# One 512-column product for both token parts in the mixers, gates and branches of a two-block layer

## The chip, the cores and the metric

The kernel runs on one core of a Trainium2 chip. The metric is the device time of one execution in microseconds; less is better. The engines are named as in the profile: PE is TensorE (its weight loads are listed as PEld), DVE is VectorE, ACT is ScalarE, POOL is GpSimd, SP issues most of the DMAs.

## The reference

256 tokens of width 2048 pass through two blocks in float32.

```python
def first_block(x, ...):
    proj = rms_norm(x, g_mix) @ w_in
    y_dsa  = dsa_mixer(q, k, v, q_idx, k_idx, w_idx)      # 8 heads, keys picked by an indexer
    y_rwkv = rwkv7_mixer(r, d_w, k, v, d_a, d_g)          # 16 heads, recurrence over the tokens
    x = x + concat([y_dsa, y_rwkv]) @ w_out
    return x + hier_moe(rms_norm(x, g_ffn), ...)          # 16 experts, group routing

def second_block(x, ...):
    proj = rmsnorm(x, norm1_g) @ w_in                     # columns: u, v | s5 | q, k, v | 3 x 2048 gates
    gates = sigmoid(proj[..., o_c:] + b_gate)
    y_a = gmlp_mixer(uv); y_b = s5_mixer(s5_in); y_c = stick_breaking_attention(q, k, v)
    br = einsum('blnw,nwd->blnd', stack([y_a, y_b, y_c]), w_branch)
    x = x + sum(gates * br) @ w_out
    x = x + square(relu(rmsnorm(x, norm2_g) @ w_mlp_in)) @ w_mlp_out
    return rmsnorm(x, final_g)
```

`s5_mixer` ends with `g * sigmoid(g @ w_glu + b_glu)`. Inside `rwkv7_mixer` the columns r, k and v are first mixed with those of the token before.

## The kernel before, in words

**Products in two parts.** Each float32 operand of a large product is split into a high part, rounded for the fast matmul, and a low part, the rest. `load_split` loads a chunk of weights (`raw`, 4 x 128 rows by 256 columns), ACT copies it into the high part (`wh`, L211) and DVE subtracts for the low part (`wl`, L212). `wh` and `wl` have three buffers each. A chunk is called a split below. The tokens are split once per block into `hx`, where for each of 16 row tiles the high 256 columns and the low 256 columns lie side by side.

**`ws_steps`** computes 256 output columns for the 256 tokens. For each row tile `k` and each of two pieces of 128 output columns it makes three products of 256 columns: `wh` with the high tokens, `wh` with the low tokens, `wl` with the high tokens. Both pieces lie in the halves of one PSUM bank (`acc`, four banks). A caller reads that bank with one DVE instruction.

**`wide_group`**, used in the MLP alone before, gives each piece a bank of its own. `wh` goes with high and low tokens side by side in one product of 512 columns, and `wl` with the high tokens in one of 256, which is added to the bank's first half. The bank's second half is then copied by ACT (`lo`, L2122) and added to the first by DVE (`r`, L2123).

**The order.** The code runs as generators: a stream of dense groups (`rkv`, `scores`, `attend` and, in block 2, `U`, `C`, `Q`, `gate`) yields after each row tile, and side chains (the rwkv chunks, attention heads, the s5 states) are advanced between the yields. A scheduler then lays all instructions out for each engine, and every engine works through its own list in order.

**Places that the prediction speaks of.** At the end of block 1 the last rwkv pair, the last attention heads and the output product (`acc<-wh,yx`) meet; then the router turns 16 tiles of the residual (`mx<-cst_cg,xr`, L1202), copies each with ACT or DVE (`hT`) and multiplies it by the router's weights (`mx<-wr,hT`). In block 2, `s5` first computes its tables on DVE (from `xm` to `ek` and `bb`), then its pool "s5" is opened with a load of `cc` on POOL's queue, and 32 states follow, each with products on PE, a scan on DVE and multiplications on POOL (`b`, `z`, `tab`, `sl`). The last product of a state is `mx<-sl,Ch`.

Of the kernel before, what the change touches and what calls it, by code (L numbers as in the profile page):

```python
# [18 lines left out]
T = 256  # L19
# [94 lines left out]
class Ker:  # L114
# [152 lines left out]
    def wide_group(self, ap, xx):  # L267
# [11 lines left out]
        return banks  # L279

# [181 lines left out]
    def mixers1(self, y, st):  # L462
# [46 lines left out]
        self.hhl = (hh, hl)  # L509

# [22 lines left out]
        def rkv(n, off, j):  # L533
            v, b = yield from self.ws_steps([(w_in[:, R0 + off + 256 * j:R0 + off + 256 * (j + 1)], 0)], 256,
                                            hh, hl, [(0, 128), (128, 128)])
            ready[n, j] = self.shift(wp, v, [mu("mu_" + n, 2 * j + i) for i in range(2)],
                                     128, bank=b[0], name=n)
# [110 lines left out]
    def shift(self, pool, views, mus, m, bank=None, name="lo"):  # L648
# [4 lines left out]
        p = bank.rearrange("p (a t) -> p a t", a=2) if n == 2 else views[0][:, None, :]  # L653
        pn = pool.tile([128, 2, T], F32, name="shn")
        nc.vector.tensor_mul(pn[:m, :n], p[:m], self.row[:m, :n])
# [284 lines left out]
    def dsa(self, y, st, chains):  # L940
        nc, A, c, par = self.nc, self.A, self.c, self.par
        hh, hl = self.hhl
        w_in = A["w_in"][0]
# [12 lines left out]
        def turned(bank, n, h, scale=1.0, src=None):  # L956
# [5 lines left out]
            for a in range(0, 128, h):  # L962
                b = a ^ h
                o, f = slice(a, a + h), slice(b, b + h)
                nc.scalar.activation(sw[o, :n * T], bank[f], AF.Copy, scale=scale if scale == 1.0 else scale[f])
            if src is bank:
                nc.scalar.activation(src, src, AF.Copy, scale=scale)
# [18 lines left out]
        two = [(0, 128), (128, 128)]  # L986
# [32 lines left out]
        def scores(j):  # L1019
            v, bk = yield from self.ws_steps([(w_in[:, 3072 + 256 * j:3328 + 256 * j], 0)], 256, hh, hl, two)  # L1020
            chains.append(scores_chain(j, bk))

        def scores_chain(j, bk):
            src, sw = turned(bk[0], 2, 32)
# [38 lines left out]
        def attend(j):  # L1063
            qk = []
            for base, gain, nm in ((0, "q_gain", "qr"), (1024, "k_gain", "kr")):
                v, bk = yield from self.ws_steps([(w_in[:, base + 256 * j:base + 256 * (j + 1)], 0)], 256, hh, hl, two)
                chains.append(qk_chain(bk, gain, nm, qk))
            chains.append(heads_chain(j, qk))

        def qk_chain(bk, gain, nm, qk):  # L1070
            src = d2.tile([128, 2 * T], F32, name="rsrc")
            nc.vector.tensor_mul(src.rearrange("p (a t) -> p a t", a=2), bk[0].rearrange("p (a t) -> p a t", a=2), self.row)
# [429 lines left out]
    def block2(self):  # L1502
        nc, A, tc = self.nc, self.A, self.tc
        w_in = A["w_in_2"][0]
        two = [(0, 128), (128, 128)]
        with ExitStack() as st:
# [5 lines left out]
            hh, hl = self.hhl  # L1512
# [6 lines left out]
            def gate(d, pool, n, ci):  # L1519
# [3 lines left out]
                v, bk = yield from self.ws_steps([(w_in[:, c0:c0 + 256], 0)], 256, hh, hl, two)  # L1523
                nc.vector.tensor_mul(*(t.rearrange("p (a t) -> p a t", a=2) for t in (g, bk[0])), row)
# [62 lines left out]
            yh = q.tile([128, 24, T], F32R, name="y2h")  # L1587
            yl = q.tile([128, 24, T], F32R, name="y2l")
# [7 lines left out]
            def glu():  # L1596
                g = q.tile([128, KD, T], F32R, name="gs", tag="ml")
                gh, gl = g[:, 0:8], g[:, 8:16]
# [3 lines left out]
                for j in range(4):  # L1602
                    v, bk = self.ws_group([(A["s5_w_glu_2"][0, :, ts(j, 256)], 0)], 256,
                                          [gh[:, k] for k in range(8)], [gl[:, k] for k in range(8)], two)
# [4 lines left out]
                    sg = q.tile([128, 2, T], F32, name="sgl", tag="m", bufs=2)  # L1609
                    for i in range(2):  # L1610
                        ct = 2 * j + i
                        nc.scalar.activation(sg[:, i], v[i], AF.Sigmoid, bias=par["b_glu"][:, ct:ct + 1])
# [598 lines left out]
```

## Time and profile before

| what | value |
|---|---|
| median of 3 runs | 2908.3 us (2908.26 to 2910.01) |
| the profiled execution's own time | 2907.5 us |
| its span | 2905.7 us |
| PE busy | 2837.3 us, 98% |
| DVE, ACT, POOL busy | 69%, 56%, 13% |

The time is 1.8 us more than the span, which runs from the first instruction to the end of the last. Busy shares are means over stages with different limits, so a stage is read from its own stretch.

### The profile page before, as it was taken

The numbers are of one execution on the slowest core, as the hardware profiler recorded it, in microseconds if no ns is written. First come the engines' busy times: TensorE is split into PE (matmuls) and PEld (weight loads), VectorE is DVE, ScalarE is ACT, GpSimd is POOL, SyncE is SP. The second block draws the span as 40 slices with busy tenths as digits, with TensorE's granted clock in tenths as the row PEclk, the third lists the DMA queues.
The fourth block names the chain that finished last, engine by engine and source line by source line (L and its number), as shares of the span: only waits on it lengthen the run. The fifth ranks groups of instructions, "written<-read, shape, count | busy, mean of one in ns | idle before, by whom it ended". The sixth has DMA issues, their size and how long they took to land.

```text
span 2905.7 us, 45911 instructions
## 1 busy us (share of the span) xinstructions
PE 2837.3 (98%) x17602; PEld 2511.7 (86%) x17602; DVE 2009.7 (69%) x2807; ACT 1628.0 (56%) x2225; POOL 371.6 (13%) x645
## 2 busy tenths in 40 slices
PE   8999999997999999999999999999999999999998
PEld 8998989876888788888878999999988888888887
DVE  7685876656898899987787866555555654456554
ACT  6455466546777777766555464444445543355443
POOL 2111111011000000015998400000000000000000
PEclk9999999998999999999999999999999999999999
DMA  7444443483989999945334456666656666666665
GB/s 204 130 117 120 118 119 100 134 278 128 372 297 338 378 382 359 381 141 165 117 105 131 140 172 186 186 189 184 187 184 199 189 189 195 192 187 187 191 193 172
DMA packets 400515, 576.68 MB, mean 198 GB/s; under 512 B 25064, under 2 KB 252656, under 8 KB 400160
## 3 DMA queue, kind: packets, MB, share of 16 engines
q1 hardware_dynamic: 397632, 567.74, 60.5%
q0 software_dynamic: 2624, 5.93, 0.7%
q8 instruction: 139, 2.28, 0.3%
q14 instruction: 88, 0.72, 0.1%
q10 hardware_dynamic: 32, 0.01, 0.0%
HBM read 571.51 MB, written 2.10 MB: 197 GB/s over the span
## 4 chain that ended last, share of the span: by engine, by line
PE 48%; POOL 6%; DVE 1%; DMA 1%; issue 0%; ACT 0%; ACTq 0%; POOLq 0%
PE acc L221 46%; PE mx L221 1%; POOL ttmp L1998 1%; POOL ttmp L2001 1%; POOL tab L1999 1%; POOL tab L2002 1%; POOL tab L2000 1%; POOL b L2037 1%; POOL z L2038 0%; POOL tab L1997 0%; POOL sl L2050 0%; DVE wl L212 0%; DMA raw<-in_w_in_dram 0%; DMA cc<-in_s_c_im_dram 0%; POOL cf L1981 0%
## 5 line engine op out<-in xcount | busy, mean ns | idle before, releaser
L212 DVE TENSOR_TENSOR wl<-raw,wh 128x1024 fp32r<-128x1024 f32 (+1 forms) x917 | 1123.6, 1229 | 651.7 <-ACT wh L211 630.2
L211 ACT ACTIVATE wh<-raw 128x1024 fp32r<-128x1024 f32 (+1 forms) x917 | 965.4, 1055 | 900.8 <-PE acc L221 718.8
L221 PE MATMUL acc<-hx,wh 128*128 128x256 f32 (+3 forms) x5280 | 1144.3, 306 | 1.7 <-ACT wh L211 1.1
L221 PEld LDWEIGHTS acc<-hx,wh 128*128 128x128 f32 (+2 forms) x5280 | 844.9, 188 | 55.2 <-issue 8.0
L221 PE MATMUL acc<-hx,wl 128*128 128x256 f32 x3152 | 886.8, 283 | 1.1 <-DVE wl L212 1.1
L221 PEld LDWEIGHTS acc<-hx,wl 128*128 128x128 f32 x3152 | 591.2, 188 | 9.9 <-issue 4.3
L212 DVE TENSOR_TENSOR wl<-rx,wh 128x1024 fp32r<-128x1024 f32 x159 | 191.4, 1223 | 26.8 <-ACT wh L211 18.5
L221 PE MATMUL acc<-wl,xgh 128*128 128x512 f32 x512 | 203.0, 398 | 1.7 <-DVE wl L212 1.4
L221 PE MATMUL acc<-wh,xgh 128*128 128x512 f32 x512 | 201.4, 394 | 2.2 <-ACT wh L211 2.1
L221 PE MATMUL acc<-wh,xgl 128*128 128x512 f32 x512 | 201.5, 394 | 0.0
L221 PE MATMUL acc<-wh,al 128*128 128x512 f32 x512 | 199.2, 389 | 0.0
L221 PE MATMUL acc<-wh,ah 128*128 128x512 f32 x512 | 199.2, 389 | 0.0
L211 ACT ACTIVATE wh<-rx 128x1024 fp32r<-128x1024 f32 x159 | 167.5, 1060 | 56.4 <-PE acc L221 38.4
L221 PE MATMUL acc<-wl,ah 128*128 128x512 f32 x512 | 179.2, 389 | 0.0
L221 PE MATMUL mx<-wh,act 128*128 128x512 f32 x512 | 138.1, 390 | 1.5 <-DVE act L218 0.8
L221 PE MATMUL acc<-wh,hx 128*128 128x512 f32 x384 | 128.7, 416 | 0.8 <-ACT wh L211 0.8
L221 PEld LDWEIGHTS acc<-wl,xgh 128*128 128x128 f32 x512 | 96.3, 188 | 26.0 <-DVE wl L212 5.5
L221 PEld LDWEIGHTS acc<-wh,xgh 128*128 128x128 f32 x512 | 96.3, 188 | 23.9 <-ACT wh L211 4.1
L221 PEld LDWEIGHTS mx<-wh,act 128*128 128x128 f32 x512 | 95.8, 188 | 22.2 <-DVE act L218 1.2
L221 PEld LDWEIGHTS acc<-wh,xgl 128*128 128x128 f32 x512 | 96.4, 188 | 20.9
L221 PEld LDWEIGHTS acc<-wh,ah 128*128 128x128 f32 x512 | 96.1, 188 | 20.0
L221 PEld LDWEIGHTS acc<-wl,ah 128*128 128x128 f32 x512 | 96.1, 188 | 19.9
(611 smaller groups left out, 4053.8 us busy)
## 6 DMA issues: line engine op xcount, KB each, us to landing
raw<-in_w_in_dram SPq DMA_DIRECT2D x304, 512.0 KB, 3.7
raw<-in_w_mlp_in_dram SPq DMA_DIRECT2D x128, 512.0 KB, 3.7
raw<-in_w_mlp_out_dram SPq DMA_DIRECT2D x128, 512.0 KB, 4.4
raw<-in_w_e_gate_dram SPq DMA_DIRECT2D x80, 512.0 KB, 6.1
raw<-in_w_e_down_dram SPq DMA_DIRECT2D x77, 512.0 KB, 5.6
raw<-in_w_e_up_dram SPq DMA_DIRECT2D x75, 512.0 KB, 5.8
raw<-in_w_out_dram SPq DMA_DIRECT2D x57, 512.0 KB, 4.3
rx<-in_w_e_up_dram SPq DMA_DIRECT2D x53, 512.0 KB, 5.9
```

The lines of the kernel that those rows point to most:

```text
L211: self.lasth = nc.scalar.activation(h[:, :n], raw[:, :n], AF.Copy).ins
L212: self.lastl = nc.vector.tensor_sub(l[:, :n], raw[:, :n], h[:, :n].bitcast(F32)).ins
L221: return self.nc.tensor.matmul(out, lhsT, rhs, start=start, stop=stop)
L1998: G.tensor_mul(tmp[:, :, :n], s0, ei)
L1999: G.tensor_sub(c1, c1, tmp[:, :, :n])
L2000: G.tensor_mul(s1, s0, er)
L2001: G.tensor_mul(tmp[:, :, :n], c0, ei)
L2002: G.tensor_add(s1, s1, tmp[:, :, :n])
L2037: G.tensor_mul(b1, z, cb)
```

## The change

`ws_steps` is replaced by `wide_steps` (the old `wide_group` as a generator) for 12 `rkv` groups, 4 `scores`, 8 of `attend`, 4 `U`, 4 `C`, 8 of `Q`, 24 gates (16 row tiles each), 4 of `glu` and 24 branches (8 row tiles each). That is 64 groups of 16 row tiles and 28 of 8. A new helper `joined` sums the two halves of each bank: two ACT copies of 256 columns, then two DVE additions. What was one DVE instruction from PSUM (a bank times `row`, say) becomes a multiplication in SBUF after the sum. `keys`, the lora group and all products with tokens as weights (`ts_steps`) stay.

```diff
-    def wide_group(self, ap, xx):
+    def wide_steps(self, ap, xx):
         K = len(xx)
         banks = [self.pacc() for _ in range(2)]
         for k0 in range(0, K, 4):
             h, l = self.load_split([(ap[k0 * 128:(k0 + 4) * 128], 0)], 4, 256)
             for k in range(4):
                 x, end = xx[k0 + k], k0 + k == K - 1
                 for i, o in enumerate(banks):
                     self.mm(o, h[:, k, ts(i, 128)], x, start=k0 + k == 0, stop=False)
                     self.mm(o[:, 0:T], l[:, k, ts(i, 128)], x[:, 0:T], start=False, stop=end)
+                yield 0.65
         return banks
+
+    def joined(self, out, banks):
+        for i, o in enumerate(banks):
+            self.nc.scalar.activation(out[:, i], o[:, T:], AF.Copy)
+        for i, o in enumerate(banks):
+            self.nc.vector.tensor_add(out[:, i], o[:, 0:T], out[:, i])
...
         def rkv(n, off, j):
-            v, b = yield from self.ws_steps([(w_in[:, ...], 0)], 256, hh, hl, [(0, 128), (128, 128)])
-            ready[n, j] = self.shift(wp, v, ..., 128, bank=b[0], name=n)
+            b = yield from self.wide_steps(w_in[:, ...], xx)
+            ready[n, j] = self.shift(wp, b, ..., 128, name=n)
...
-            nc.vector.tensor_mul(*(t.rearrange("p (a t) -> p a t", a=2) for t in (g, bk[0])), row)
+            gv = g.rearrange("p (a t) -> p a t", a=2)
+            self.joined(gv, bk)
+            nc.vector.tensor_mul(gv, gv, row)
...
         def cols(j):
-            v, bk = yield from self.ws_steps([(w_in[:, ...], 0)], 256, hh, hl, two)
+            bk = yield from self.wide_steps(w_in[:, ...], xx)
             yj = y[:, 8 + 2 * j:10 + 2 * j]
-            V.tensor_mul(yj, bk[0].rearrange("p (a t) -> p a t", a=2), self.row)
+            self.joined(yj, bk)
+            V.tensor_mul(yj, yj, self.row)
```

On PE, at the end of block 1, these rows stand between the last product of the output projection (`acc<-wl,yx`) and the router's last products, before:

```order
L221 MATMUL acc<-wl,yx 128x512
L221 MATMUL mx<-wr,hT 128x20 x6
L1202 MATMUL mx<-cst_cg,xr 128x128 x6
L221 MATMUL mx<-wr,hT 128x20 x2
L1202 MATMUL mx<-cst_cg,xr 128x128 x2
L221 MATMUL mx<-wr,hT 128x20 x2
L1202 MATMUL mx<-cst_cg,xr 128x128 x2
L221 MATMUL mx<-wr,hT 128x20 x4
L1202 MATMUL mx<-cst_cg,xr 128x128 x2
L221 MATMUL mx<-wr,hT 128x20 x2
L1202 MATMUL mx<-cst_cg,xr 128x128 x4
```

Three more rows follow there (two, two and six of the same). Now the same place reads:

```order
L221 MATMUL acc<-wl,yx 128x512
L1220 MATMUL mx<-cst_cg,xr 128x128 x6
L221 MATMUL mx<-wr,hT 128x20 x2
L1220 MATMUL mx<-cst_cg,xr 128x128 x2
L221 MATMUL mx<-wr,hT 128x20 x6
```

Before, 9 tiles were still to be turned and 12 to be multiplied after the last dense product; now it is 4 and 4. The others stand further up, between products of the output projection.

Also on PE, a little earlier, the last chunk of the last rwkv pair (`pn,X` to `yt` and `sq`) and the last attention heads (`kr,qr`, then `P`), before:

```order
L221 MATMUL mx<-kr,qr 128x128
L221 MATMUL acc<-wh,yx 128x512 x4
L742 MATMUL mx<-gr,sa 128x64
L742 MATMUL mx<-ar,S 128x64
L742 MATMUL mx<-gkr,tm 128x64
L742 MATMUL mx<-gr,sa 128x64
L221 MATMUL acc<-wh,yx 128x512
L221 MATMUL acc<-wl,yx 128x512
```

Six more dense products follow there before `kr,qr`, `yt` and `sq`. Now there is none:

```order
L221 MATMUL mx<-kr,qr 128x128
L755 MATMUL mx<-gr,sa 128x64
L755 MATMUL mx<-ar,S 128x64
L755 MATMUL mx<-gkr,tm 128x64
L755 MATMUL mx<-gr,sa 128x64
L221 MATMUL mx<-kr,qr 128x256
L221 MATMUL mx<-yt,cst_c_250 128x512
L224 MATMUL mx<-cst_cg,P 128x128 x3
L221 MATMUL mx<-sq,cst_c_250 128x512
```

The very last head stands a few rows further on:

```order
L221 MATMUL mx<-kr,qr 128x256
L224 MATMUL mx<-cst_cg,P 128x128 x3
L221 MATMUL mx<-PT,V 128x256
```

Twelve dense products that stood between `pn,X` and `yt` have moved up, and in the last piece the last head's `P` follows its `kr,qr` with nothing between.

On DVE, at the start of block 2, the s5 tables (`pk`, `sc`, `ek`, `bb`) stand between the splits (`wl`), before:

```order
L212 TENSOR_TENSOR wl<-raw,wh 128x1024
L1867 TENSOR_TENSOR pk<-pk,den 32x128
L1869 TENSOR_TENSOR t_13572<-ar,lim 32x128
L1870 TENSOR_TENSOR pk<-pk,t_13572 32x128
L1926 TENSOR_TENSOR y_13469<-acc,row 128x512
L1871 TENSOR_TENSOR pk<-pk,den 32x128
L212 TENSOR_TENSOR wl<-raw,wh 128x1024
L1876 COPY sc<-mx 128x160
```

And now:

```order
L212 TENSOR_TENSOR wl<-raw,wh 128x1024
L1888 TENSOR_TENSOR pk<-pk,t_12920 32x128
L290 TENSOR_TENSOR y_12817<-acc,y_12817 128x256
L1889 TENSOR_TENSOR pk<-pk,den 32x128
L1891 TENSOR_TENSOR t_12920<-ar,lim 32x128
L1948 TENSOR_TENSOR y_12817<-y_12817,row 128x512
L1892 TENSOR_TENSOR pk<-pk,t_12920 32x128
L212 TENSOR_TENSOR wl<-raw,wh 128x1024
L1893 TENSOR_TENSOR pk<-pk,den 32x128
L212 TENSOR_TENSOR wl<-raw,wh 128x1024
L1898 COPY sc<-mx 128x160
```

The additions of `joined` (L290) stand among the tables, and splits have moved ahead of them: from the start of block 2 to the last row of the tables there were 18 splits, and there are 21 now.

## Rows read from the trace of the kernel before

**Rows 1.** The profile page, parts 1 and 2, over the whole span.

```profile
span 2905.7 us, 45911 instructions
PE 2837.3 (98%) x17602; PEld 2511.7 (86%) x17602; DVE 2009.7 (69%) x2807; ACT 1628.0 (56%) x2225; POOL 371.6 (13%) x645
...
POOL 2111111011000000015998400000000000000000
PEclk9999999998999999999999999999999999999999
```

**Rows 2.** Stretches: us, busy of PE, PEld, DVE, ACT, POOL (instructions), PEclk, DMA, GB/s.

```profile
1730.00:1830.00 100.00, 100.00 (x852) 100.00 (x851) 63.21 (x68) 49.47 (x62) 0.00 (x0) 1.00 0.61 186
...
2250.00:2370.00 120.00, 120.00 (x685) 104.83 (x684) 73.62 (x86) 62.16 (x86) 0.00 (x0) 1.00 0.61 188
...
1337.00:1555.00 218.00, 199.59 (x1338) 176.00 (x1337) 175.90 (x330) 124.95 (x256) 202.84 (x404) 0.93 0.40 122
1555.00:1600.00 45.00, 42.65 (x303) 37.91 (x302) 33.96 (x64) 23.11 (x45) 32.57 (x62) 1.00 0.42 123
...
620.00:690.00 70.00, 54.44 (x277) 47.10 (x276) 32.32 (x74) 28.91 (x51) 8.35 (x6) 0.80 0.58 205
```

**Rows 3.** Chain that ended last, 1330 to 1620 us, share by line.

```profile
by line: PE acc L221 21.3%; POOL ttmp L1998 7.8%; POOL ttmp L2001 7.5%; POOL tab L1999 7.4%; PE mx L221 6.8%; POOL tab L2002 6.2%; POOL tab L2000 5.7%; POOL b L2037 5.6%; POOL z L2038 4.7%; POOL tab L1997 4.7%; POOL sl L2050 4.1%; issue 3.6
```

**Rows 4.** PE in order of time: a gate's products, then the MLP's.

```profile
1900.29 0.40 PE L221 MATMUL acc<-hx,wh 128*128 128x256 f32 x2
1900.52 0.28 PE L221 MATMUL acc<-hx,wl 128*128 128x256 f32 x1
...
2300.42 0.40 PE L221 MATMUL acc<-hx,wh 128*128 128x512 f32 x1
2300.65 0.28 PE L221 MATMUL acc<-hx,wl 128*128 128x256 f32 x1
```

**Rows 5.** DVE in order of time: reading a gate's bank, an MLP group's banks.

```profile
1803.32 0.69 DVE L1524 TENSOR_TENSOR g<-acc,row 128x512 f32<-128x512 f32 x1 [0.63 <-PE acc L221]
...
2091.64 0.69 DVE L1524 TENSOR_TENSOR g<-acc,row 128x512 f32<-128x512 f32 x1 [0.62 <-PE acc L221]
...
2201.13 0.42 DVE L2123 TENSOR_TENSOR r<-acc,lo 128x256 f32<-128x256 f32 x1
...
2369.43 0.42 DVE L2123 TENSOR_TENSOR r<-acc,lo 128x256 f32<-128x256 f32 x1 [0.64 <-ACT lo L2122]
```

**Rows 6.** Lines L2122, L2123 and L1635: ns min/median/max.

```profile
L2122 ACT ACTIVATE lo<-acc x64: 362/380/387, 2200.6 to 2724.0; 128x256 f32<-128x256 f32 x64
...
L2123 DVE TENSOR_TENSOR r<-acc,lo x64: 415/418/425, 2201.1 to 2725.3; 128x256 f32<-128x256 f32 x64
...
L1635 DVE TENSOR_TENSOR m<-m,g x16: 691/693/693, 1758.8 to 2098.0; 128x512 f32<-128x512 f32 x16
```

**Rows 7.** PE in order of time, end of block 1, router.

```profile
656.80 0.39 PE L221 MATMUL acc<-wl,yx 128*128 128x512 f32 x1
657.04 1.41 PE L221 MATMUL mx<-wr,hT 128*128 128x20 f32 x12
...
665.13 2.59 PE L221 MATMUL mx<-wr,hT 128*128 128x20 f32 x12
```

**Rows 8.** ACT in order of time, router.

```profile
667.16 2.56 ACT L1280 ACTIVATE nx<-xr,rs 128x512 fp32r<-128x512 f32 x4
669.62 0.19 ACT L1146 ACTIVATE sge<-sge 128x8 f32<-128x8 f32 x1
```

**Rows 9.** PE in order of time, last chunk and heads; idle before in brackets.

```profile
578.36 0.59 PE L221 MATMUL mx<-kr,qr 128*128 128x256 f32 x2
...
582.38 0.28 PE L224 MATMUL mx<-cst_cg,P 128*128 128x128 f32 x1
...
584.92 0.92 PE L221 MATMUL mx<-PT,V 128*128 128x256 f32 x4 [0.98 <-ACT PT L1110]
...
593.51 1.12 PE L221 MATMUL mx<-sq,cst_c 128*128 128x512 f32 x2 [1.40 <-ACT sq L921]
...
597.89 0.92 PE L221 MATMUL mx<-PT,V 128*128 128x256 f32 x4 [0.58 <-ACT PT L1110]
...
599.74 0.50 PE L221 MATMUL acc<-wh,yx 128*128 128x512 f32 x1 [0.92 <-ACT yx L217]
```

**Rows 10.** POOL in order of time, its start in s5; PE, the 24th state.

```profile
1337.47 0.95 POOL L1916 DMA_DIRECT2D cc<-in_s_c_re_dram  x1 [39.52 <-ACT wh L211]
...
1595.94 0.22 PE L221 MATMUL mx<-sl,Ch 128*64 128x128 f32 x1
```

**Rows 11.** POOL line L2037; DVE line L212 from 1400 to 1550 us.

```profile
L2037 POOL TENSOR_TENSOR b<-z,tab x32: 721/770/1819, 1369.9 to 1672.6; 128x256 f32<-128x256 f32 x32
...
L212 DVE TENSOR_TENSOR wl<-raw,wh x35: 1194/1226/1750, 1400.4 to 1548.8; 128x1024 fp32r<-128x1024 f32 x35
```

More of the change, by code (lines that the diff above doesn't have):

```diff
@@ L533, in rkv @@
         def rkv(n, off, j):
[L534 to L537, printed above, removed]
+            b = yield from self.wide_steps(w_in[:, R0 + off + 256 * j:R0 + off + 256 * (j + 1)], xx)
+            ready[n, j] = self.shift(wp, b, [mu("mu_" + n, 2 * j + i) for i in range(2)], 128, name=n)
         def dense():
@@ L652, in shift @@
         o = pool.tile([128, 2, T], F32, name="sh_" + name, bufs=2 if name == "v" else 1)
-        p = bank.rearrange("p (a t) -> p a t", a=2) if n == 2 else views[0][:, None, :]
         pn = pool.tile([128, 2, T], F32, name="shn")
-        nc.vector.tensor_mul(pn[:m, :n], p[:m], self.row[:m, :n])
+        if n == 2:
+            self.joined(pn, views)
+            nc.vector.tensor_mul(pn, pn, self.row)
+        else:
+            nc.vector.tensor_mul(pn[:m, :n], views[0][:m, None, :], self.row[:m, :n])
         p = pn
@@ L964, in turned @@
                 o, f = slice(a, a + h), slice(b, b + h)
-                nc.scalar.activation(sw[o, :n * T], bank[f], AF.Copy, scale=scale if scale == 1.0 else scale[f])
-            if src is bank:
+                nc.scalar.activation(sw[o, :n * T], bank[f], AF.Copy, scale=scale if isinstance(scale, float) else scale[f])
+            if src is bank and not isinstance(scale, float):
                 nc.scalar.activation(src, src, AF.Copy, scale=scale)
@@ L1019, in scores, with sums, scores_chain @@
         def scores(j):
[L1020 to L1024, printed above, removed]
+            bk = yield from self.wide_steps(w_in[:, 3072 + 256 * j:3328 + 256 * j], xx)
+            chains.append(scores_chain(j, sums(bk)))
+        def sums(bk):
+            o = dp.tile([128, 2 * T], F32, name="qs", bufs=3)
+            self.joined(o.rearrange("p (a t) -> p a t", a=2), bk)
+            return o
+        def scores_chain(j, src):
+            src, sw = turned(src, 2, 32, 1.0, src)
             qi = d2.tile([128, 2, T], F32, name="qi")
@@ L1065, in attend, with qk_chain @@
             for base, gain, nm in ((0, "q_gain", "qr"), (1024, "k_gain", "kr")):
-                v, bk = yield from self.ws_steps([(w_in[:, base + 256 * j:base + 256 * (j + 1)], 0)], 256, hh, hl, two)
-                chains.append(qk_chain(bk, gain, nm, qk))
+                bk = yield from self.wide_steps(w_in[:, base + 256 * j:base + 256 * (j + 1)], xx)
+                chains.append(qk_chain(sums(bk), gain, nm, qk))
             chains.append(heads_chain(j, qk))
-        def qk_chain(bk, gain, nm, qk):
-            src = d2.tile([128, 2 * T], F32, name="rsrc")
-            nc.vector.tensor_mul(src.rearrange("p (a t) -> p a t", a=2), bk[0].rearrange("p (a t) -> p a t", a=2), self.row)
+        def qk_chain(src, gain, nm, qk):
+            sv = src.rearrange("p (a t) -> p a t", a=2)
+            nc.vector.tensor_mul(sv, sv, self.row)
             sq = d2.tile([128, 2 * T], F32, name="qsq")
@@ L1602, in glu @@
                 for j in range(4):
-                    v, bk = self.ws_group([(A["s5_w_glu_2"][0, :, ts(j, 256)], 0)], 256,
-                                          [gh[:, k] for k in range(8)], [gl[:, k] for k in range(8)], two)
+                    bk = self.wide_group(A["s5_w_glu_2"][0, :, ts(j, 256)],
+                                         [g[:, k].rearrange("p a t -> p (a t)") for k in range(8)])
                     if held:
@@ L1721, in sb @@
         hh, hl = self.hhl
-        two = [(0, 128), (128, 128)]
+        xx = self.hx
         V = None
@@ L1742, in attend @@
             for i, (base, sc) in enumerate(((3072, 128 ** -0.5), (4096, 1.0))):
[L1743 to L1745 removed]
+                bk = yield from self.wide_steps(w_in[:, base + 256 * j:base + 256 * (j + 1)], xx)
+                bi = both[:, 2 * i:2 * i + 2]
+                self.joined(bi, bk)
+                nc.vector.scalar_tensor_tensor(bi, bi, sc, self.row, op0=OP.mult, op1=OP.mult)
             chains.append(heads(j, both[:, 0:2], both[:, 2:4], pre))
@@ L2119, in mlp @@
                     r = p.tile([128, 512], F32, name="r", bufs=2)
[L2120 to L2123 removed]
+                    self.joined(r.rearrange("p (a t) -> p a t", a=2), banks)
                     nc.scalar.activation(r, r, AF.Relu)
```

59 lines of the change are left out of this document (27 added, 32 removed).

## The prediction

> **What bounds the kernel now.** I read the page first: PE is busy for 2837.3 of 2905.7 us, and POOL is busy in two places only [rows 1]. So the reader looks for what PE does with its time where it is full, and for the stretches where it is not. Then the stretches: from 1730 to 1830 us, in gates and branches, PE is busy for all 100 us, and its weight loads (PEld) too; in the MLP PE is full as well, while PEld has 104.83 of 120 us [rows 2]. The two stretches where PE has gaps and a lower granted clock are 620 to 690 us (54.44 of 70 us, clock 0.80) and 1337 to 1555 us (199.59 of 218 us, clock 0.93) [rows 2]. The clock has the levels 2.4 and 1.2 GHz, so 0.80 is a mean over both. The first stretch is the router. In the second POOL is busy for 202.84 of 218 us, and the chain that ended last runs there mostly through POOL's lines [rows 2, 3]: the s5 states. Everywhere else an instruction on DVE or ACT costs nothing unless PE has to wait for it.
>
> **The change part by part.** My sum has four terms.
>
> *First, PE's stream.* Each pair of row tile and piece had three products of 256 columns and gets one of 512 and one of 256. The columns stay 768, so only what a product costs beside its columns can go. From one start to the next, two products of 256 columns take 1900.52 - 1900.29 = 0.23 us and one of 512 takes 2300.65 - 2300.42 = 0.23 us [rows 4]; those stamps are too coarse, so I take whole groups. From the gate's bank read at 1803.32 to that at 2091.64 there are 17 rounds of one gate and one branch, (16 + 8) x 2 = 48 pairs each: 16.96 / 48 = 353.3 ns a pair [rows 5]. From 2201.13 to 2369.43 there are 15 MLP groups of 32 pairs: 11.22 / 32 = 350.6 ns [rows 5]. The difference is 2.7 ns. The change touches 64 groups of 32 pairs and 28 of 16, 2496 pairs: 6.7 us. Eight of these groups (256 pairs, 0.7 us) end between 1337 and 1596 us, where POOL sets the pace, and gain nothing there: -6.0 us. Bounds: 0, if the difference between the stretches comes from something else, and 6.7.
>
> *Second, the new instructions.* Each of the 92 groups adds two ACT copies (380 ns) and two DVE additions (418 ns) [rows 6]; `scores` loses one ACT copy. That is 70 us of ACT and 77 us of DVE in the whole kernel, where both have hundreds free [rows 1]. They hold up splits: a copy waits for its bank's last product, and the next `wh` stands behind it; an addition waits for the copy, and `wl` stands behind it. In the MLP the same four instructions stand among the same splits and PE is full [rows 2], because a split is made three buffers ahead of its use. A group now takes two of four banks, so the group after the next waits for them; the shortest groups are branches, a third of 16.96 us or 5.65 us, and a drain is 2 x 0.38 + 2 x 0.42 us and a split or two, so it is done. I cost this at nothing in the gates and branches; without that cover it would be 0.8 us for each group.
>
> *Third, the end of block 1*, where the scheduler's lists differ. Before, the router still had 9 tiles to turn and 12 to multiply after the last dense product at 656.80; its last products start at 665.13 and take 2.59, so 10.9 us lie behind the dense stream [rows 7]. Now 4 tiles remain. With 12 tiles in 10.9 us, 0.9 us each, 8 fewer would give 7.3 us. But the ACT list behind them holds a table load and four `nx` copies before `sge` at 669.62 [rows 8], and the last residual must be added and squared first; that does not shrink. I take -4.7 us (bounds 0 and -7.3).
>
> Against that, the last rwkv chunk and the last heads. Twelve dense products of 0.23 us (2.8 us) that covered the step from `pn,X` to `yt` stand earlier now, and the last head's `P` follows `kr,qr` with nothing between. An earlier head took from 578.36 to 582.38 for this, 4.0 us with other work in it [rows 9]. So between 0 and 6.8 us of new waiting; the four gaps of 0.98, 1.40, 0.58 and 0.92 us that stand there already [rows 9] show that such steps are waited for once cover is gone. I take the middle, +3.5.
>
> *Fourth, s5.* POOL starts its part at 1337.47, when the tables are done [rows 10]. Three more splits now stand before the last of them, and PE uses up one split in 16.96 / 6 = 2.83 us: POOL starts 8.5 us later in PE's work. Then each of the eight groups in that stretch multiplies by `row` from SBUF and SBUF instead of from PSUM and SBUF. POOL's `b` takes between 721 and 1819 ns for one and the same shape, and a split there up to 1750 ns where it mostly takes 1226 [rows 11]: the two engines hold each other up. One such multiplication takes 691 ns [rows 6], so POOL loses between 0 and 8 x 0.69 = 5.5 us. The Trainium skill, "SBUF — State Buffer", section "Who interferes with whom", says why: a DVE instruction with two SBUF inputs contends with a GpSimd instruction that reads SBUF, one with a PSUM input does not. The trace's spread agrees, and the rule speaks against this change: by it alone the full 5.5 us would be added to the sum, 2908 us. By the rows most instructions are not held up (median 770 against 721 ns), and part of it falls into slack.
>
> Is the lateness made up? The 24th state ends on PE at 1595.94 [rows 10], 258.5 us after POOL's start; POOL was busy in it for at most 202.84 + 32.57 = 235.4 [rows 2], so 23 us are slack. In the new list the first states stand about 10 us of dense products later and the 24th at the very same dense product, so PE does early what it did between the states. A start 8.5 us later with 5.5 us more work, 14 us, still fits in 23 us. Bounds 0 and +14; I take +2.
>
> Sum: -6.0 - 4.7 + 3.5 + 2.0 = -5.2 us. The profiled execution took 2907.5 us, so 2902.3; it lies 0.8 us under the median of 2908.3, so for a median I say 2903 us.
>
> **The rivals.** *POOL's lateness is not made up* (the other side). Place: the states from 1337 us on. If PE waits for each state as late as POOL starts and is slowed, +14 stands in place of +2; and if the additions, in order on DVE ahead of each scan, put their 0.84 us into the chain for each of the eight groups, another 6.7: -6.0 - 4.7 + 3.5 + 20.7 = +13.5, 2921.8 us. It decides from a lateness of 13 us at the 24th state on (13 - 7.2 = 5.8). For it: POOL is busy for 93% of the stretch. Against it: the slack after 1555 us, where POOL is busy for 32.57 of 45 us [rows 2].
>
> *The end of block 1 is covered anyway.* If the heads' and chunk's waits hide under what PE has, and s5 loses nothing: -6.0 - 4.7 = -10.7, 2897.6 us. For it: the largest gap there was 1.40 us, so the chains nearly keep up. Against it: there are four such gaps already, with more cover than now [rows 9].
>
> *The weight loads set PE's pace.* For it: PEld is full in the gates [rows 2]. Then a third fewer loads would save 353.3 / 3 = 118 ns a pair, 294 us: 2614 us. Against it: the MLP has two loads a pair, PEld 87%, and the same pace to 0.8% [rows 2, 5]. The Trainium skill, "TensorE: Matmul & The Clock Gate", section "Back-to-back issue gap", gives about 81 ns for a pair of load and product of 128 columns and 131 ns for 512, by which a product of 512 would be far cheaper than two of 256; no row here shows it.
>
> *The change gives nothing on PE and the drains are waited for:* 92 groups with 0.8 us, +74 us, 2982 us. Against it stands the full PE in the MLP.
>
> **How the numbers follow.** A measurement of this kernel tells about 0.2% (5.8 us) from no change: faster is below 2902.5, slower above 2914.1. Forecast 0.62, with its own range 2898 to 2908, the terms a few us off either way; 0.27 of it is faster, 0.35 the same. POOL not made up 0.14, of which 0.03 would still be within 5.8 us. Block 1 covered 0.19, faster. Weight loads 0.01, drains 0.04. So faster 0.47, same 0.38, slower 0.15. The range leaves out the far cases and most of the slow one: 2893 to 2915.
>
> **What would show it.** Rounds of a gate and a branch at 16.83 us instead of 16.96, with PE at 100%; PEld below 90% there. The router's last products within 6 us behind the last dense one instead of 10.9. Two or three new gaps of 1 to 2.5 us at `yt`, `P` and `PT,V` before it. POOL's start in s5 later against the dense stream, and the 24th state no more than 2 us later than the rest of the kernel would have it. It would be wrong if rounds stay at 16.96, if the gates show PE waiting for `g` or `m`, or if `mx<-sl` waits for POOL up to the 24th state.

## The result and the profile after

The changed kernel takes 2929.8 us (median of 4 runs, 2927.9 to 2933.5) where the kernel before takes 2908.3 (median of 4): a ratio of 1.0077, with a 95% interval of 1.0065 to 1.0089 (the two medians alone give 1.0074). It is 21.5 us slower; I had predicted 2903 us, and 2915 as the upper end of my range.

The page of the changed kernel, parts 1 and 2, beside [rows 1]:

```profile
span 2931.7 us, 41263 instructions
PE 2850.0 (97%) x15106; PEld 2400.8 (82%) x15106; DVE 2084.0 (71%) x2991; ACT 1675.2 (57%) x2404; POOL 385.4 (13%) x645
...
POOL 1111101011000000014898510000000000000000
PEclk9999999998999999999999999999999999999999
```

PE issues 2496 products fewer, as the change says, but it is busy 12.7 us longer, and the span has grown by 26.0. So the time has gone into gaps, and into products that take longer.

To find the place I lined the two traces up by dense work: for each share of the columns of all products with `wh` or `wl`, when does PE get there? The columns are the same in both kernels. Worked out from the starts of the products in both traces:

| share of dense columns | before, us | after, us | later by |
|---|---|---|---|
| 2% | 69.0 | 73.5 | 4.4 |
| 15% (last heads of block 1 begin) | 575.1 | 575.7 | 0.7 |
| 18% (first expert's products) | 711.0 | 725.7 | 14.7 |
| 38% (last expert) | 1228.7 | 1243.9 | 15.2 |
| 39% (last products of block 1) | 1256.3 | 1273.1 | 16.8 |
| 39.2% (first dense product of block 2) | 1270.2 | 1288.0 | 17.8 |
| 52% (first late gates) | 1714.4 | 1742.7 | 28.3 |
| 68% (branches end) | 2113.1 | 2139.0 | 26.0 |
| 98% (MLP) | 2849.0 | 2874.9 | 26.0 |

Two places lose most of it: the end of block 1 and the stretch of the s5 states (10.5 us from block 2's first dense product to 52%). Gates and branches win 2.3. My expectations below take the 39% mark for the start of block 2, which is why they have 11.5 us for that stretch. At the end of block 1 the table shows 14 us from 15% to 18%. But 4.4 us are there by 2% already, and the mark at 15% hides them, because chain products that stood ahead of it before stand behind it now (shown below); so some 10 us arise at the end of block 1. The run with `RS` at 4.1 below has the list of the kernel before on PE up to block 2, and its trace is 4.3 us late at 2% too. Whether these 4.4 us belong to the change is therefore not shown; the profiled execution took 2933.5 us, 3.7 more than the median.

**End of block 1.** PE in order of time in the changed kernel, idle before in brackets; [rows 9] and [rows 7] are the same place before.

```profile
591.02 1.12 PE L221 MATMUL mx<-pn,X 128*128 128x128 f32 x4 [2.62 <-ACT pn L895]
...
598.93 0.44 PE L224 MATMUL mx<-cst_cg,P 128*128 128x128 f32 x2 [1.03 <-DVE P L1120]
...
603.95 0.49 PE L221 MATMUL mx<-kr,qr 128*128 128x128 f32 x2 [0.47 <-ACT y L1133]
...
608.41 0.33 PE L224 MATMUL mx<-cst_cg,P 128*128 128x128 f32 x1 [0.52 <-DVE P L1114]
610.27 0.44 PE L224 MATMUL mx<-cst_cg,P 128*128 128x128 f32 x2 [1.53 <-DVE P L1120]
611.29 1.33 PE L221 MATMUL mx<-PT,V 128*128 128x256 f32 x4 [0.58 <-ACT PT L1128]
613.54 2.50 PE L221 MATMUL acc<-wh,yx 128*128 128x512 f32 x5 [0.92 <-ACT yx L217]
...
676.81 0.40 PE L221 MATMUL acc<-wl,yx 128*128 128x512 f32 x1
677.05 0.27 PE L1220 MATMUL mx<-cst_cg,xr 128*128 128x128 f32 x1
...
679.84 1.41 PE L221 MATMUL mx<-wr,hT 128*128 128x20 f32 x12
```

Eight steps of the last chains are waited for, where it was four. The output product that needs the last head starts at 613.54 instead of 599.74, 13.8 us later, of which 13.1 have arisen since 15%. The gaps explain 4 of them (8.2 us in this stretch, with one of 0.52 before `sa,tm`, against 3.9 before). The stretches of both kernels, columns as in [rows 2], show the rest. The kernel before:

```profile
580.00:600.00 20.00, 16.12 (x90) 12.11 (x89) 10.72 (x29) 7.59 (x19) 0.05 (x1) 1.00 0.18 53
600.00:616.00 16.00, 15.71 (x68) 12.31 (x68) 9.54 (x14) 8.39 (x10) 6.38 (x10) 1.00 0.99 318
```

The changed kernel:

```profile
580.00:600.00 20.00, 15.84 (x74) 12.03 (x73) 12.19 (x26) 9.47 (x17) 0.00 (x0) 0.83 0.21 62
600.00:616.00 16.00, 11.98 (x42) 7.84 (x41) 7.19 (x21) 5.06 (x13) 5.29 (x9) 0.86 0.56 185
```

The granted clock was 0.83 and 0.86 instead of 1.00. As a mean of the levels 2.4 and 1.2 GHz that is 6.8 and 4.5 us at the lower level, which costs at most half of it, 5.6 us (an estimate from these rows); the last 2.5 us of the slow time lie behind 613.54, so up to 4.4 us of the cost count here. The remaining 4 us are work that the mark at 15% hides: up to this output product both traces have 1440 chain products on PE, but 98 of them stand behind the mark now and 76 before. So that lateness had arisen earlier, and it is as large as the 4.4 us at 2%.

**The s5 states.** What PE waited for there, in us, times and longest; the kernel before from 1337 to 1742 us:

```profile
PE mx L221 <- POOL sl L2050: 12.2, 9, 2.8
PE mx L221 <- ACT zsb L1773: 2.4, 1, 2.4
PE mx L1972 <- ACT rc L1966: 2.2, 1, 2.2
PE mx L221 <- ACT sh L2049: 1.5, 1, 1.5
PE mx L221 <- DVE mxd L1706: 1.2, 2, 0.7
PE acc L221 <- ACT wh L211: 0.8, 1, 0.8
PE acc L221 <- DVE wl L212: 0.3, 1, 0.3
```

And the changed kernel from 1354 to 1770 us:

```profile
PE mx L221 <- POOL sl L2072: 14.5, 7, 3.5
PE mx L221 <- DVE Bl L218: 4.3, 4, 1.8
PE mx L221 <- DVE mxd L1727: 3.2, 2, 1.8
PE mx L1994 <- ACT rc L1988: 2.2, 1, 2.2
PE acc L221 <- DVE wl L212: 1.8, 4, 0.6
PE acc L221 <- ACT wh L211: 1.0, 1, 1.0
PE mx L1991 <- DVE zsc L1792: 0.4, 1, 0.4
```

20.6 us of waits have become 27.4, spread over POOL (`sl`) and steps of the chains on DVE (`Bl`, `mxd`) alike. That is 6.8 of the 10.5 us. The same stretches, columns as in [rows 2], first before and then changed:

```profile
1337.00:1742.00 405.00, 384.23 (x2804) 351.15 (x2803) 316.25 (x569) 227.67 (x423) 269.40 (x507) 0.96 0.44 133
1354.00:1770.00 416.00, 387.84 (x2237) 323.87 (x2236) 332.11 (x616) 236.47 (x459) 276.81 (x507) 0.95 0.43 130
```

The clock is at its lower level for 30.7 us of the first stretch and 37.6 of the second by its records in the two traces. That costs up to 3.4 us more (an estimate), most of what the waits leave. Where [rows 10] has POOL's start and a late state, the changed kernel has

```profile
1361.53 0.95 POOL L1938 DMA_DIRECT2D cc<-in_s_c_re_dram  x1 [44.98 <-PE acc L221]
```

```profile
1618.85 0.27 PE L221 MATMUL mx<-sl,Ch 128*64 128x128 f32 x1
```

They come 24.1 and 22.9 us later, where block 2 began 17.8 later.

**Gates and branches, MLP.** The changed kernel in two full stretches, columns as in [rows 2]:

```profile
1756.00:1856.00 100.00, 100.00 (x572) 87.37 (x571) 74.10 (x97) 58.60 (x95) 0.00 (x0) 1.00 0.62 190
2276.00:2396.00 120.00, 120.00 (x685) 104.84 (x684) 73.62 (x86) 62.13 (x86) 0.00 (x0) 1.00 0.62 188
```

And two readings of a gate's banks on DVE that lie 17 rounds apart, where [rows 5] has the kernel before:

```profile
1830.87 0.42 DVE L290 TENSOR_TENSOR g<-acc,g 128x256 f32<-128x256 f32 x1 [0.63 <-ACT g L288]
...
2117.75 0.42 DVE L290 TENSOR_TENSOR g<-acc,g 128x256 f32<-128x256 f32 x1 [0.67 <-ACT g L288]
```

A round takes 286.88 / 17 = 16.875 us instead of 16.96, with PE full and PEld down from 100% to 87%. That part of the change works.

### The profile page after: what moved, and what is told of

It reads as the page before. It is cut to its first block, busy times and chain, and to the rows that moved or that the text cites. A ratio compares the mean times of both kernels' runs of the same rounds, so it can differ in the third digit from the quotient of the medians.

```text
span 2931.7 us, 41263 instructions
## 1 busy us (share of the span) xinstructions
PE 2850.0 (97%) x15106; PEld 2400.8 (82%) x15106; DVE 2084.0 (71%) x2991; ACT 1675.2 (57%) x2404; POOL 385.4 (13%) x645
## 4 chain that ended last, share of the span: by engine, by line
PE 46%; POOL 7%; DVE 2%; issue 1%; ACT 1%; DMA 0%; ACTq 0%; POOLq 0%; DVEq 0%
PE acc L221 45%; PE mx L221 1%; POOL tab L2024 1%; POOL tab L2022 1%; POOL ttmp L2020 1%; POOL ttmp L2023 1%; POOL b L2059 1%; POOL tab L2021 1%; POOL sl L2072 1%; POOL z L2060 1%; POOL tab L2019 1%; DVE wl L212 1%; DMA raw<-in_w_in_dram 0%; ACT wh L211 0%; POOL tc L2001 0%
## 5 line engine op out<-in xcount | busy, mean ns | idle before, releaser
L212 DVE TENSOR_TENSOR wl<-raw,wh 128x1024 fp32r<-128x1024 f32 (+1 forms) x917 | 1125.6, 1232 | 594.2 <-ACT wh L211 577.0
L221 PE MATMUL acc<-hx,wh 128*128 128x512 f32 (+2 forms) x3232 | 1125.2, 394 | 0.8 <-DVE hx L357 0.8
L221 PEld LDWEIGHTS acc<-hx,wh 128*128 128x128 f32 (+1 forms) x3232 | 595.1, 188 | 129.0 <-issue 6.1
L212 DVE TENSOR_TENSOR wl<-rx,wh 128x1024 fp32r<-128x1024 f32 x159 | 191.7, 1225 | 29.6 <-ACT wh L211 21.3
L221 PE MATMUL acc<-y,wh 128*128 128x512 f32 x384 | 135.5, 395 | 0.0
```

Source lines behind the costliest of these rows:

```text
L212: self.lastl = nc.vector.tensor_sub(l[:, :n], raw[:, :n], h[:, :n].bitcast(F32)).ins
L221: return self.nc.tensor.matmul(out, lhsT, rhs, start=start, stop=stop)
```

## The experiments

**Theory at the start, "two places"**: the last heads of block 1 and the s5 states lose all of it, and the other groups win a little. **Rival, "drains everywhere"**: the copies and additions of `joined` cost 21.5 / 92 = 0.23 us in each group. All kernels of this part are the kernel before with the change in some of the groups. All ratios are to the kernel before on the same chip. The code cuts are shortened; from the run without the products on, they show the difference to the run with which the text compares.

**Block 1 alone** (`rkv`, `scores`, `attend`):

```diff
         def rkv(n, off, j):
+            b = yield from self.wide_steps(w_in[:, ...], self.hx)
...
         def scores(j):
+            bk = yield from self.wide_steps(w_in[:, ...], self.hx)
+            chains.append(scores_chain(j, sums(bk)))
...
         def attend(j):
+                bk = yield from self.wide_steps(w_in[:, ...], self.hx)
+                chains.append(qk_chain(sums(bk), gain, nm, qk))
```

> The change in block 1's 24 groups alone (12 of r, k and v, 4 of scores, 8 of queries and keys); block 2 as before. Theory 'two places': in the changed kernel the first expert product comes 14.7 us later against the same amount of dense work, and all of that arose between 575 and 640 us, where the last heads' chain is later and its cover has run out. So all of it stays here: 2908.3 + 14.7 = 2923 us, between 2919 and 2926. Rival 'drains everywhere': the 21.5 us are the price of the added copies and additions, 0.23 us for each of 92 groups; then 24 groups cost 5.6 us: 2914 us.

Measured: 2919.1 us, ratio 1.0047 (1.0029 to 1.0064), +11.3. By dense work it is 2.1 us early at 15% and 10.9 late at 18%, and it stays there. Two places holds; drains everywhere would have given 5.6.

**U, C and Q alone**, these lines in `U` and `cols`, and alike in the stick-breaking `attend`:

```diff
+            bk = yield from self.wide_steps(w_in[:, ...], self.hx)
+            self.joined(yj, bk)
+            nc.vector.tensor_mul(yj, yj, self.row)
```

> The change in the 16 groups U, C and Q of block 2 alone. Theory 'two places': the changed kernel loses 11.5 us between 1256 and 1740 us of the kernel before, where POOL starts its s5 part 7.2 us later against what went before and PE waits for the states all the way; so +9 to +12 here, 2917 to 2920 us, with POOL's first instruction of that part some 7 us later than in the kernel before. Rival 'drains everywhere': 16 of 92 groups, +3.7 us, 2912 us. My prediction's own term (lateness made up by the 24th state): +2 less 0.7, 2910 us.

Measured: 2913.2 us, 1.0017 (1.0007 to 1.0027), +5.4. POOL's start lies 72.5 us behind the first dense product of block 2 instead of 67.3, so 5.2 us later; yet by dense work only some 4 us are lost from 38% to 52%, and of the 5.9 us of this trace 4.5 are there before block 2's first dense product, up to which PE's list is that of the kernel before. Both theories miss: the median is less than the changed kernel loses here and more than 3.7, and what the trace shows behind that product is 1.4 us.

**Gates, glu and branches alone**, in `gate`, and alike in `glu` and `branch`:

```diff
+                bk = yield from self.wide_steps(w_in[:, c0:c0 + 256], self.hx)
+                self.joined(gv, bk)
+                nc.vector.tensor_mul(gv, gv, row)
```

> The change in gates, glu and branches alone (24 groups of 16 row tiles, 28 of 8: 1216 pairs). Theory 'two places': no place loses here and the pair is 2.7 ns shorter, -3.3 us: 2905 us, between 2903.5 and 2907, and a round of a gate and a branch is 16.83 us. Rival 'drains everywhere': 52 of 92 groups, +12 us, 2920 us. A weaker rival: the gates that stand among the s5 states delay POOL's chain too, +2 to +4 us: 2907 to 2909 us.

Measured: 2907.9 us, 1.0001 (0.9991 to 1.0010). Drains everywhere falls here: 52 of 92 groups cost nothing. In the trace it ends 1.2 us early, after 0.7 late at 38%: 1.9 us won from there on. That is less than 3.3, because a pair wins less than I thought (below).

**r, k and v alone**, the first of block 1's edits:

```diff
         def rkv(n, off, j):
+            b = yield from self.wide_steps(w_in[:, ...], self.hx)
```

> The change in block 1's 12 groups of r, k and v alone. Theory 'the heads' chain': what is lost at the end of block 1 comes from the queries and keys, whose chain is the one that ends last there; r, k and v are early, and their lateness is gone in the list of products by 260 us of dense work. So -1.0 us (384 pairs by 2.7 ns): 2907.3 us, between 2906 and 2909. Rival: each of the 24 groups of block 1 adds to the lateness alike; then 12 of them cost half of 14.7, 2915.6 us.

Measured: 2910.7 us, 1.0012 (1.0003 to 1.0022), +2.9, against 7.3 by the rival. In the trace the end of block 1 lies 2.5 us later and the end of the kernel 0.7. The median is over my range, and its interval lies above 1, so r, k and v are not shown to be free.

**Scores, queries and keys alone**, the other two:

```diff
+            bk = yield from self.wide_steps(w_in[:, ...], self.hx)
+            chains.append(scores_chain(j, sums(bk)))
...
+                chains.append(qk_chain(sums(bk), gain, nm, qk))
```

> The change in block 1's scores, queries and keys alone (12 groups), r, k and v as before. Theory 'the heads' chain': the end of block 1 is lost here and nowhere else, so nearly the whole of block 1's +11 us stays: 2917 to 2920 us, with the last kr in the traces some 20 us later and the first w_out product 10 to 14 us later than in the kernel before. Rival: r, k and v and the heads add up (r, k and v alone gave +2.9 in the median): 8 us, 2915 us.

Measured: 2919.7 us, 1.0040 (1.0026 to 1.0054), +11.6: all of block 1's loss. Now the place was clear, and I split this edit into its two halves.

**Its instructions without its products:**

```diff
-            bk = yield from self.wide_steps(...)
+            v, bk = yield from self.ws_steps(...)
...
+            for i in range(2):
+                nc.scalar.activation(ov[:, i], bk[0][:, ts(i, T)], AF.Copy, scale=0.0)
+            for i in range(2):
+                nc.vector.tensor_add(ov[:, i], bk[0][:, ts(i, T)], ov[:, i])
```

> Products of block 1 as before (three of 256 columns, both pieces in one bank), but scores, queries and keys are read from the bank by the changed kernel's two copies and two additions (the copies are scaled by zero, so that the sum stays right) and multiplied by row in a step of its own. Theory 'instructions': it is the four more instructions of each group on ScalarE and VectorE that make the heads' chain late, so +8 to +11 us, 2916 to 2919 us. Rival 'products': the wide products in two banks of four let PE run ahead of the chain, and the instructions are nothing: 2908 to 2910 us. Both alike: +5, 2913 us.

Measured: 2910.3 us, 1.0007 (0.9997 to 1.0017), +2.2.

**Its products without its instructions:**

```diff
-            self.joined(o.rearrange("p (a t) -> p a t", a=2), bk)
+            for i in range(2):
+                nc.vector.tensor_mul(o[:, ts(i, T)], bk[i][:, 0:T], self.row[:, i])
```

> The counterpart: scores, queries and keys with the changed kernel's wide products in two banks, but of each bank only the first half is read, by one multiplication with row (one copy for scores); the product of the weight's first part with the token's second part is left out of the sum. So the products of the change without its added instructions. Theory 'instructions': nothing is late, 384 pairs by 2.7 ns: 2907 us, 2905 to 2910. Rival 'products': +8 to +11, 2916 to 2919 us.

Measured: 2909.0 us, 1.0005 (0.9995 to 1.0015), +0.9. Neither half costs what the whole costs, so neither theory is right: 2.2 + 0.9 is far from 11.6. Both halves also change the order of work; whether that is the cause, the runs with another list test.

**Later copies.** In the wide heads the copies stand at the group's end, ahead of chain steps on ACT's list. They were moved into the chain:

```diff
-                chains.append(qk_chain(sums(bk), gain, nm, qk))
+                chains.append(qk_chain(bk, gain, nm, qk))
...
         def qk_chain(src, gain, nm, qk):
+            src = sums(src)
```

> Scores, queries and keys wide as in the run with these alone (+11.6 us), but the copies and additions are written in the first step of the chain that uses the sum, not at the group's end; TensorE's list of products is almost the same. Theory 'copies in the way': it is the copies at the group's end, which wait for the bank's last product and hold up a ready chain step behind them on ScalarE; then most is given back, +0 to +5 us, 2908 to 2913 us. Rival 'longer chain in the list': the steps stand behind more dense products in TensorE's list, whatever ScalarE does: +9 to +12, 2917 to 2920 us.

Measured: 2921.3 us, 1.0043 (1.0028 to 1.0059), +13.3. The copies in the way are not it; the rival, a longer chain in the list, had predicted +9 to +12.

**Block 2 alone** (the edits of the runs with U, C and Q and with the gates together):

> The change in block 2 alone: U, C, Q, gates, glu and branches; block 1 as before. In the changed kernel block 2 from its first dense product to the end took 8.2 us longer than before, with U, C and Q alone 1.5 us longer, with gates and branches alone 2.0 us shorter. Theory 'together': the gates that stand among the states add their drains to a chain that U, C and Q have made late already, so the two don't add up: +8 to +10, 2916 to 2918 us, and the last sl ends some 8 us later against the first dense product of block 2. Rival 'they add up': 5.4 + 0.2, 2913.5 us, and the 8.2 of the changed kernel came from that run.

Measured: 2919.5 us, 1.0039 (1.0027 to 1.0050), +11.4. U, C and Q alone gave 5.4 and the gates 0.2: together they cost twice the sum. With the 11.3 of block 1 alone, the two blocks make 22.7 us, near the 21.5 of the whole change. From 1343 to 1755 us PE waited for `sl` 16.0 us.

**Block 2 without U and C:**

> Block 2's change (+11.4 us together) without U and C: Q, gates, glu and branches wide. Theory 'late start': U and C are drained ahead of POOL's start in s5, on a VectorE that is busy for 67 of 75 us there; without them POOL starts as in the kernel before (67 us after block 2's first dense product instead of 72.6), and the time is 2908 - 3 + 0 to 2 = 2905 to 2908 us. Rival 'late states': it is the drains of Q and of the early gates, among the states, that cost: +5 to +8, 2913 to 2916 us.

Measured: 2910.0 us, 1.0006 (0.9997 to 1.0015), +2.0; POOL starts 66.0 us behind the first dense product (67.3 before). **Block 2 without the four early gates:**

```diff
+                if pool is ge:
+                    v, bk = yield from self.ws_steps(...)
+                    nc.vector.tensor_mul(gv, bk[0].rearrange(...), row)
```

> Block 2's change without the four early gates, which stand among the s5 states: U, C, Q, the late gates, glu and branches wide. Theory 'together': the early gates' drains came on top of U, C and Q and made +5.4 into +11.4; without them 5.4 - 2.9 = +2.5, 2910.5 us, 2908 to 2913. Rival: U, C and Q alone cost it, and the run with these alone came out low: +8 to +9, 2916 us.

Measured: 2910.4 us, 1.0005 (0.9996 to 1.0015), +2.4. POOL's start in this run, 72.5 us behind the first dense product of block 2:

```profile
1345.93 0.95 POOL L1936 DMA_DIRECT2D cc<-in_s_c_re_dram  x1 [43.86 <-PE acc L221]
```

and in block 2 whole, 72.6 us behind it:

```profile
1346.33 0.95 POOL L1932 DMA_DIRECT2D cc<-in_s_c_re_dram  x1 [44.88 <-PE acc L221]
```

The last of the 32 states, without the early gates and then in block 2 whole:

```profile
1693.75 0.23 PE L221 MATMUL mx<-sl,Ch 128*64 128x128 f32 x1
```

```profile
1700.74 0.22 PE L221 MATMUL mx<-sl,Ch 128*64 128x128 f32 x1
```

That is 420.3 and 427.1 us behind the first dense product of block 2, where the kernel before has 422.4. So a late start of 5 us is made up by the last state when the early gates are as before, and is not when they are wide too.

Counted from block 2's first dense product to the last instruction, the traces differ from the kernel before (1635.6 us) as follows. The lists on PE up to that product are the same in all these runs.

| wide in block 2 | us |
|---|---|
| U, C and Q | +1.4 |
| gates, glu and branches | -2.1 |
| all of it | +7.1 |
| all but U and C | -1.8 |
| all but the early gates | -1.8 |

Seven traces of kernels that leave block 2 as it was lie between -2.5 and +0.1. So each part alone is nearly free, and together they are not. These are single traces; the medians, +5.4 for U, C and Q above all, contain what arises before block 2 as well.

**Same instructions, another list.** With that left open, the last question was whether instructions or order cost the time. Two constants set how fast the code writes side chains between the dense products; changing them leaves every instruction and changes the order in which the scheduler lays them out (17218 products on PE, 2245 instructions on ACT, 2831 on DVE and 645 on POOL in both kernels of the first pair).

```diff
-    FILL, CHAIN, PREP = (4.03, 1.1, 2.53)
+    FILL, CHAIN, PREP = (4.03, 1.0, 2.53)
```

> The same instructions as the run with scores, queries and keys wide (+11.6 us), each with the same operands; only the pace constant CHAIN is 1.0 instead of 1.1, which changes the order in which the heads' chain and the dense products are written, so the scheduler's list differs from the V product on. In this list the last head's products come after less dense work and the router's tiles stand where they stood in the kernel before. Theory 'list': most of the +11.6 is gone, 2907 to 2912 us, with the last kr before 575 us instead of 587.5. Rival 'instructions': the copies and additions are there as before, so 2917 to 2921 us.

Measured: 2909.6 us, 1.0006 (0.9996 to 1.0015), +1.7 instead of +11.6, with the same instructions. The last `kr` on DVE and the first output product after the last head on PE, in the run with scores, queries and keys wide:

```profile
587.49 0.69 DVE L990 TENSOR_TENSOR kr<-qs,qsq 128x512 f32<-128x512 f32 x1
```

```profile
610.93 2.50 PE L221 MATMUL acc<-wh,yx 128*128 128x512 f32 x5 [0.92 <-ACT yx L217]
```

and here:

```profile
579.36 0.69 DVE L990 TENSOR_TENSOR kr<-qs,qsq 128x512 f32<-128x512 f32 x1 [1.36 <-ACT qsq L1097]
```

```profile
601.03 2.50 PE L221 MATMUL acc<-wh,yx 128*128 128x512 f32 x5 [0.92 <-ACT yx L217]
```

The last `kr` comes 8.1 us earlier (not before 575 us, as I had expected) and the output product 9.9 us: the whole difference between the two kernels. This `kr` is still 11.6 us later than in the kernel before (567.78), but the output product only 1.3: a late step need cost PE little as long as the list has other work ahead of the product that needs it. From the 15% mark to that output product PE stands idle for 3.3 us here and for 8.7 in the run with scores, queries and keys wide, and the clock differs too, here and there (columns as in [rows 2]):

```profile
580.00:600.00 20.00, 17.69 (x90) 12.82 (x90) 11.90 (x36) 6.97 (x17) 0.00 (x0) 0.96 0.12 34
```

```profile
580.00:600.00 20.00, 15.81 (x66) 10.60 (x65) 11.29 (x27) 7.38 (x15) 0.00 (x0) 0.74 0.16 53
```

The kernel before was not run with this constant, so what a new list would give it is open. For block 2, with the instructions of block 2 whole:

```diff
-    RS, RC = (3.9, 0.52)
+    RS, RC = (4.1, 0.52)
```

> Block 2's change whole (+11.4 us), same instructions, with RS at 4.1 instead of 3.9: the s5 states are written later, the late states some 10 to 20 us of dense products further back in TensorE's list. Theory 'list': POOL starts 5 us later, TensorE meets the states too early and waits (16.0 us for sl, 12.2 before, and 8 us more for other steps of the same chain); with more dense products ahead of each late state these waits are covered: 2908 to 2913 us. Rival 'chain too long': the later states meet the end of the dense products of this stretch and the gates wait for the last of them: 2919 us or more.

Measured: 2916.0 us, 1.0027 (1.0017 to 1.0038), +8.0 instead of +11.4, short of what I expected. Behind block 2's first dense product its trace loses 2.3 us; 6.4 stand before it, in a list that is that of the kernel before. And with `RS, RC = (3.9, 0.6)`:

> As the run before this one, but with RC at 0.6 instead of 0.52 and RS as it was: the side chains (GM, heads) are written more slowly, and the states stand 4 to 10 us of dense products earlier in the second half. Theory 'list': the states are met earlier still, so the loss stays or grows: 2919 to 2924 us. Rival: the side chains' steps on VectorE and ScalarE delay POOL's chain, and fewer of them give some back: 2913 to 2917 us.

Measured: 2922.8 us, 1.0057 (1.0041 to 1.0074), +14.8. Three lists of the same instructions give 8.0, 11.4 and 14.8 us, in the traces 2.3, 7.1 and 10.1 us behind block 2's first dense product.

**What the experiments point to**: wide products where no chain stands beside them, the late gates, glu and branches. The edit is that of the gates alone with `if pool is ge:` as above.

> Only the 20 late gates, glu and the 24 branches wide, nothing that stands beside a chain: 1088 pairs by 2.7 ns, -2.9 us: 2905.2 us, 2903.5 to 2907. Rival: the gain of the rounds is given back at glu or at the first gates (in the run with all gates 1.1 of 3.3 us were left): 2907 to 2908 us. Whether this is faster than the kernel before is at the edge of what five rounds can tell.

Measured: 2907.7 us, 0.9998 (0.9989 to 1.0007). The expected gain of 2.9 us (1.9 by the measured pair) lies inside the interval, -3.2 to +2.0 us, and so does none. In the trace 1.9 us are won between 52% and 68%, in the late gates and branches. No version that I ran is shown to be faster than the kernel before.

## Why the prediction was wrong

**PE's stream** (-6.0): right in kind, too large. The pair went from 353.3 to 16.875 us / 48 = 351.6 ns, 1.8 ns and not 2.7; for 2496 pairs 4.4 us at most. What I took as the effect of the wide product, the difference to the MLP's pair, was partly a difference between the stretches. The weight loads did not set the pace: PEld fell to 87% and the pair hardly moved. By the Trainium skill, "TensorE: Matmul & The Clock Gate", section "Back-to-back issue gap", a load and product of 512 columns take some 131 ns. [rows 4] has 0.23 us, and the measured pair of 351.6 ns speaks against it too.

**The new instructions** (0): right by themselves. 52 groups with them cost nothing measurable, and in the heads they gave 2.2 us, within the noise. But I costed them only as work and cover, not as a cause of another list.

**The end of block 1** (-4.7 + 3.5): this step failed, and is about half of the loss (some 10 us here and 11.3 in the run with block 1 alone). *The router's part*: as forecast, less than 6 us lie behind the last dense product, 4.4 (676.81 to 681.25) instead of 10.9. But from the output product that waits for the last head to the router's last product it is 67.7 us instead of 68.0 ([rows 7, 9]). PE had been busy in the 10.9 us; the products that moved up took their time there. I had priced a move as if it were a removal: 0.3 us instead of 4.7. *The lost cover*: the added gaps are 4.3 us, near my 3.5, though they lie at eight steps and not at the two that I priced. The clock, which I had not priced at all, cost up to as much again. The rest of the 13.1 us had arisen ahead of the last heads.

**s5** (+2): this failed too. The start came 24.06 us later than before, 17.8 of which were there when block 2 began: 6.2 us, where I had 8.5. POOL's 507 instructions of this part were busy for 276.81 us instead of 269.40, 7.4 more and over my bound of 5.5, but that went into slack: from its start to the first `sl` product of the state at 1595.94 before ([rows 10]; I called it the 24th, counted again it is the 23rd) it took 258.5 us, and to the same state after, at 1618.85, 257.3. By the Trainium skill, "SBUF — State Buffer", section "Who interferes with whom", a DVE instruction with two SBUF inputs contends with a GpSimd instruction that reads SBUF. The longer busy time agrees with that, but nothing of it reached the chain, against the 5.5 us by the rule alone. What failed is "is the lateness made up?": behind block 2's first dense product that state came 5.1 us late, not under 2, and the last state 6.0. The slack I counted was idle time of POOL. But PE loses time where its list has no dense products ahead of a state, and how late the states are does not tell that: without the early gates the same state comes 331.7 us behind that product, later than in block 2 whole (329.6; 325.8 before), and yet PE loses nothing behind it. Without the early gates the lateness was made up by the last state; with them it was not. Why four early gates do this is not shown; with the same instructions in other lists the loss of block 2 whole was 2.3, 7.1 and 10.1 us.

**The rivals.** "POOL's lateness is not made up" came true in so far as its place lost 10.5 us where it said 20.7, but not by its mechanism: the state is 5.1 us late and not 13. Its sum (2921.8) missed block 1. "Block 1 covered anyway" was as far off as one can be.

**What would show it**: 87% PEld, full gates and the router's last products within 6 us were all seen, and none of them was where the time went.

What stays open: why both halves of the heads' edit are needed for the bad list, what makes the first 2% of some traces up to 4.4 us longer, and whether the scheduler could be given one for the whole change that keeps the gain of PE's stream.

## What to carry to other kernels

Where a scheduler orders the work, an edit is priced by the chains whose steps move, not by its instructions: the same instructions ran 10 us apart in two lists. Work moved into a stretch where the bound engine is full is moved, not saved; look whether that engine was idle where it came from. And two edits that are nearly free alone can cost much together: try them together before adding up. When two traces are lined up, look first at a stretch that the edit left alone: what differs there is not the edit's.

## What the hardware showed that I had not expected

Waits came with a lower clock here, but not in step with their sum. In the tail of block 1 there were eight gaps of 0.47 to 2.62 us, and the granted clock was 0.83 and 0.86 over 36 us where it had been 1.00 with four gaps of up to 1.40: 8.2 us of gaps came with up to 5.6 us of slower products. But with the later copies PE stood idle longer in the same 20 us, 5.2 us against 4.2, and the clock stayed at 1.00 (from 600 to 616 us it was 0.79 there too):

```profile
580.00:600.00 20.00, 14.81 (x79) 10.26 (x78) 14.03 (x32) 9.91 (x20) 0.00 (x0) 1.00 0.18 53
```

A third fewer weight loads took PEld from 100% to 87% in the gates and gave 0.5% of a round.
